# Attention of the second layer: twelve bursts on TensorE in a written order, and two multiplications on GpSimd

## The chip, the cores and the metric

The kernel runs on one core of a Trainium2 chip. The metric is the device time of one execution in microseconds, and the number for a kernel is the median of its runs. The engines are named as the profile names them: PE (TensorE matmuls), PEld (its weight loads), DVE (VectorE), ACT (ScalarE), POOL (GpSimd), SP (SyncE, which issues the loads).

## What is computed

Two decoder layers work on 256 tokens of width 1024, in float32. Layer 0 mixes tokens by causal pooling, layer 1 by causal attention with 12 heads of width 64; both layers also attend with 4 heads to a memory of 256 rows, and both end in a squared-ReLU MLP of width 4096. With 256 tokens there is one block of keys, so the block choice of the reference always takes the token's own block, and layer 1 is plain causal attention:

```python
def moba_mixer(qkv, q_gain, k_gain, cos, sin):
    q, k, v = jnp.split(qkv, 3, axis=-1)
    ...
    q = apply_rope(rms_norm(heads(q), q_gain), cos, sin)
    k = apply_rope(rms_norm(heads(k), k_gain), cos, sin)
    ...
    s_own = jnp.einsum('bhcd,bhkd->bhck', qc, k_own).astype(jnp.float32) * scale
    s_own = jnp.where(kpos[None, :] <= qpos[:, None], s_own, NEG)
    ...
    p = jax.nn.softmax(s, axis=-1).astype(v.dtype)
    ...
x = x + jnp.concatenate([tok, mo], axis=-1) @ w_out[i]
u = rms_norm(x, g_mlp[i])
x = x + jnp.square(jax.nn.relu(u @ w_ff1[i])) @ w_ff2[i]
```

## The kernel before, in words

Tokens lie on the 128 partitions in two blocks, `b` = 0 and 1. A float32 product is made of three fp32r matmuls: every operand is split into a rounded part `hi` and a rest `lo`, and `mm3` (L142 to L145) adds hi by hi, hi by lo and lo by hi into one PSUM accumulator `acc`. Weights come by DMA into `raw` (seven buffers), ACT makes `hi` (L132, or L136 with the gain as scale) and DVE makes `lo` (L133, L139); sixteen buffers of each let both run ahead of PE. The activations of layer 1 are `x2T`.

The attention of layer 1 needs five column chunks of `w_in_moba`, each 512 wide. `in_chunk` (L222) makes a chunk in eight steps, k = 0 to 7, of six matmuls (three parts by two token blocks), so a chunk is 48 matmuls. In order: chunk 2048 (values of heads 8 to 11 and memory queries), three chunks of queries and keys of four heads each (`qk_chunk(0)` to `qk_chunk(2)`), and chunk 1536 (values of heads 0 to 7). Then `wout_phase` (L391) multiplies the concatenated heads `cat` with `w_out`, 96 matmuls, the first four steps of 12 in the written order and the rest accumulator by accumulator; every finished accumulator is added to `xr` and transposed (`residual_t`, L162).

Between these projections stand small pieces of work, which `in_chunk` calls as hooks at steps that the table `PLAN` gives:

- `mem_q` (L284): four transposes of the memory queries, and their split.
- `mem_scores` (L337): 12 matmuls per token block, maximum on DVE, `exp` on ACT straight from PSUM.
- `qk_evac` (L714): after a chunk of queries and keys, for each block, squares on ACT (L202), sums on DVE (L204), the power -1/2 on POOL (`rsqrt`, L189), rotation on DVE (L722 to L726), then the keys' half of `rot` times the factors on DVE (L727), four transposes on PE (L730) and a copy to `qkT` on ACT (L731).
- `tok_scores` (L736): four score products per block for four heads; they are float32 and show as eight PE rows in the trace. `tok_probs` (L748) adds the mask and takes the maximum on DVE (L753), then calls `exp_t`.
- `exp_t` (L308): `exp` with its sum on ACT (L314), the reciprocal of the sum on DVE (L318), the probabilities times it on DVE (L321), and, held back in `pend` until `later` or `flush` calls it, transposes on PE (L327) and a copy to `pT` on ACT (L332). For four heads of the token attention that makes 8 `exp`, 8 multiplications (four of 128x128, four of 128x256) and 12 transposes.
- `av_out` (L357): probabilities times values, and the split of the result into `cat` (L150 on ACT, L151 on DVE).

`pend` holds at most `LAG` = 2 entries. All small pieces share four PSUM tiles (`psp`), the projections four accumulators (`accp`).

The order of instructions on PE, ACT, DVE and POOL is not the order of the program text: the framework's scheduler sets it when the kernel is built. Only SP (and ACT at the start) follow the program, under `manual_schedule`. Whatever the order, each engine works its own list one by one, and waits on semaphores.

Of the kernel before, what the change touches and what calls it, by code (L numbers as in the profile page):

```python
# [10 lines left out]
F32 = mybir.dt.float32  # L11
# [7 lines left out]
P = 128  # L19
# [17 lines left out]
LAG = 2  # L37

PLAN = {'x': 6, 'q': 5, 'bw': 7, 'pool': 5, 'mem0': (2, 4, 6, 6),
        'mem1': (7, 8), 'tok0': (5, 6), 'tok1': (0, 6), 'tok2': (6, 8), 'out2': 8,  # L40
        'bands': ((0, 2), (1, 1), (3, 5), (4, 4)), 'group': (2, 0, 4), 'outs': (0, 4),
        'wout0': (2, 4, 5, 6, 0, 1, 7, 3), 'wout1': (6, 7, 0, 2, 1, 4, 3, 5)}
# [11 lines left out]
def trunk(ctx: ExitStack, tc: tile.TileContext, x, mem, x_t0, x_t, mem_t, small, bands, rope, mask,  # L54
# [229 lines left out]
    def mem_q(a, b, qT):  # L284

        q = st.tile([P, MEMW], F32, tag="mq", name=nm("mq"))
        nc.scalar.activation(q, a, AF.Copy)
        ss = head_sums(a, 4)
        ps = psum("mem_q")
# [4 lines left out]
        return ss  # L294


    pend = []

    def later(fn):
        pend.append(fn)  # L300
        while len(pend) > LAG:
            pend.pop(0)()

    def flush():
        while pend:
            pend.pop(0)()

    def exp_t(pool, entries, p, nbuf, put):  # L308
# [82 lines left out]
    def wout_phase(l, order, catT, gcol):  # L391
        a = [[accum(), accum()], [accum(), accum()]]
        tail = []
        for i, k in enumerate(order):
            pieces = wout_rows(l, k, a, catT, gcol + k if gcol is not None and k < 6 else None)
# [298 lines left out]
    with tc.tile_pool(name="l1", bufs=1) as lp:  # L694
# [19 lines left out]
        def qk_evac(a, b, i):  # L714
# [12 lines left out]
            nc.vector.tensor_tensor(heads(rot[:, 256:]), heads(rot[:, 256:]), bcast(r[:, 4:], 4), op=ALU.mult)  # L727
            ps = psum("qk_evac")
            for c in range(4):
                nc.tensor.transpose(ps[:, c * P:(c + 1) * P], rot[:, c * P:(c + 1) * P], ident)  # L730
            nc.scalar.activation(qkT[:, 4 * i:4 * i + 4, b * P:(b + 1) * P],  # L731
                                 ps.rearrange("p (c t) -> p c t", c=4), AF.Copy)
# [15 lines left out]
        def tok_probs(b, h0, ps, nk, qr):  # L748
            s = lp.tile([P, 512], F32, tag="s", name=nm("s"), bufs=3)
# [8 lines left out]
            def put(pT):  # L758
                for j in range(2):
# [27 lines left out]
        steps = mem_heads(cat, mq, mk1, mqa, lp, (3, 6))
        qk_chunk(0, list(zip(PLAN['mem1'], steps)))
        steps[2]()
        for i in (1, 2):  # L790
            qk_chunk(i, list(zip(PLAN[f'tok{i - 1}'], head_scores(4 * i - 4))))
        hooks = list(zip(PLAN['tok2'], head_scores(8))) + [(PLAN['out2'], lambda: (later(lambda: tok_out(8)), flush()))]
# [102 lines left out]
```

## Time and profile before

| what | us |
|---|---|
| median of three runs (558.42 to 558.80) | 558.58 |
| the profiled execution's own time | 558.29 |
| its span, first to last instruction | 556.1 |
| busy in the span: PE | 548.4 |
| busy: DVE | 391.0 |
| busy: ACT | 358.7 |
| busy: POOL | 25.0 |

The span is what the trace covers; the profiled execution took 2.2 us more than it, outside any instruction. Busy times are unions of an engine's instructions, so overlapping instructions count once. The durations of matmuls are modelled, and consecutive ones overlap: how long one holds PE is read from the distance of two starts, not from its duration.

### The profile page before, as it was taken

The numbers are of one execution on the slowest core, as the hardware profiler recorded it, in microseconds if no ns is written. First come the engines' busy times: TensorE is split into PE (matmuls) and PEld (weight loads), VectorE is DVE, ScalarE is ACT, GpSimd is POOL, SyncE is SP. The second block draws the span as 40 slices with busy tenths as digits, with TensorE's granted clock in tenths as the row PEclk, the third lists the DMA queues.
The fourth block names the chain that finished last, engine by engine and source line by source line (L and its number), as shares of the span: only waits on it lengthen the run. The fifth ranks groups of instructions, "written<-read, shape, count | busy, mean of one in ns | idle before, by whom it ended". The sixth has DMA issues, their size and how long they took to land.

```text
span 556.1 us, 8168 instructions
## 1 busy us (share of the span) xinstructions
PE 548.4 (99%) x2883; PEld 456.5 (82%) x2883; DVE 391.0 (70%) x795; ACT 358.7 (64%) x658; POOL 25.0 (4%) x27
## 2 busy tenths in 40 slices
PE   8999999999999999999999999999999999999997
PEld 5888687888888888888877777878888888888885
DVE  5798977684764945948969999565858477485462
ACT  6889967756656566565767887657665665656510
POOL 0102100000000000000012112000000000000000
PEclk9999999999999999999999999999999999999999
DMA  8989674365736648449473344352584483663301
GB/s 285 340 303 342 217 222 147 100 200 195 250 121 233 183 153 271 139 164 292 147 234 111 103 149 130 119 169 78 176 278 124 180 281 104 222 227 118 147 0 75
DMA packets 46567, 101.93 MB, mean 183 GB/s; under 512 B 3648, under 2 KB 11584, under 8 KB 46528
## 3 DMA queue, kind: packets, MB, share of 16 engines
q1 hardware_dynamic: 46384, 101.42, 55.1%
q8 instruction: 22, 0.36, 0.3%
q14 instruction: 17, 0.14, 0.1%
q10 hardware_dynamic: 144, 0.01, 0.0%
HBM read 100.37 MB, written 1.05 MB: 182 GB/s over the span
## 4 chain that ended last, share of the span: by engine, by line
PE 91%; ACT 4%; DMA 1%; DVE 1%; POOL 1%; issue 0%; SPq 0%
PE step L448 18%; PE acc L143 18%; PE acc L144 17%; PE acc L145 17%; PE step L451 10%; PE acc L448 3%; ACT hi L136 2%; PE exp_t L327 2%; PE av_out L367 2%; PE acc L451 1%; PE tok_scores L743 1%; PE transpose L162 1%; DMA raw<-in_w_in_pool_dram 1%; POOL r L189 1%; PE qk_evac L730 1%; ACT junk L182 1%
## 5 line engine op out<-in xcount | busy, mean ns | idle before, releaser
L136 ACT ACTIVATE hi<-raw,sm 128x512 fp32r<-128x512 f32 (+1 forms) x212 | 149.2, 723 | 53.0 <-PE acc L145 28.1
L139 DVE SCALAR_TENSOR_TENSOR lo<-raw,sm,hi 128x512 fp32r<-128x512 f32 x212 | 150.6, 749 | 18.2 <-ACT hi L136 17.3
L132 ACT ACTIVATE hi<-raw 128x512 fp32r<-128x512 f32 (+1 forms) x152 | 94.2, 632 | 71.2 <-PE acc L145 63.1
L143 PE MATMUL acc<-hi,hh 128*128 128x512 f32 x256 | 99.9, 390 | 0.0
L144 PE MATMUL acc<-lo,hh 128*128 128x512 f32 x256 | 99.8, 390 | 0.0
L145 PE MATMUL acc<-hi,hl 128*128 128x512 f32 x256 | 99.8, 390 | 0.0
L133 DVE TENSOR_TENSOR lo<-raw,hi 128x512 fp32r<-128x512 f32 (+1 forms) x152 | 95.1, 689 | 0.0
L432 DVE TENSOR_TENSOR r<-step,c 128x256 f32<-128x256 f32 x56 | 23.6, 422 | 98.5 <-ACT c L431 98.5
L145 PEld LDWEIGHTS acc<-hi,hl 128*128 128x128 f32 x256 | 48.1, 188 | 10.1
L143 PEld LDWEIGHTS acc<-hi,hh 128*128 128x128 f32 x256 | 48.1, 188 | 9.5
L144 PEld LDWEIGHTS acc<-lo,hh 128*128 128x128 f32 x256 | 48.1, 188 | 9.5
L448 PE MATMUL step<-x1T,hi 128*128 128x512 f32 x224 | 51.9, 389 | 0.0
L448 PE MATMUL step<-x3T,hi 128*128 128x512 f32 x224 | 51.9, 389 | 0.0
L448 PEld LDWEIGHTS step<-x1T,hi 128*128 128x128 f32 x224 | 42.0, 188 | 8.7
L448 PEld LDWEIGHTS step<-x3T,hi 128*128 128x128 f32 x224 | 42.0, 188 | 8.7
L431 ACT ACTIVATE c<-step 128x256 f32<-128x256 f32 x56 | 21.3, 381 | 19.4 <-PE step L451 19.4
L143 PE MATMUL acc<-hi,x2T 128*128 128x512 f32 x80 | 32.2, 402 | 0.0
L145 PE MATMUL acc<-hi,x2T 128*128 128x512 f32 x80 | 31.7, 396 | 0.0
L144 PE MATMUL acc<-lo,x2T 128*128 128x512 f32 x80 | 31.6, 394 | 0.0
L451 PEld LDWEIGHTS step<-x3T,lo 128*128 128x128 f32 x224 | 27.8, 192 | 0.5
L451 PEld LDWEIGHTS step<-x1T,lo 128*128 128x128 f32 x224 | 27.8, 192 | 0.5
L451 PE MATMUL step<-x1T,lo 128*128 128x256 f32 x224 | 28.0, 283 | 0.0
(151 smaller groups left out, 755.3 us busy)
## 6 DMA issues: line engine op xcount, KB each, us to landing
raw<-in_w_ff_dram SPq DMA_DIRECT2D x128, 512.0 KB, 4.8
raw<-in_w_out_dram SPq DMA_DIRECT2D x16, 512.0 KB, 4.5
raw<-in_w_in_moba_dram SPq DMA_DIRECT2D x24, 256.0 KB, 4.5
raw<-in_w_mem_kv_dram SPq DMA_DIRECT2D x8, 512.0 KB, 5.6
raw<-in_w_in_moba_dram SPq DMA_DIRECT2D x8, 512.0 KB, 5.0
raw<-in_w_in_pool_dram SPq DMA_DIRECT2D x7, 512.0 KB, 6.3
xr<-in_x_dram SPq DMA_DIRECT2D x2, 512.0 KB, 7.5
raw<-in_mem_t_dram SPq DMA_DIRECT2D x4, 256.0 KB, 6.7
```

What stands on the lines that cost most here:

```text
L132: nc.scalar.activation(hi, raw, AF.Copy)
L133: nc.vector.tensor_tensor(lo, raw, hi.bitcast(F32), op=ALU.subtract)
L136: last_hi[0] = nc.scalar.activation(hi[:, :m], raw[:, :m], AF.Copy, scale=g)
L139: nc.vector.scalar_tensor_tensor(lo, raw, g, hi.bitcast(F32), op0=ALU.mult, op1=ALU.subtract)
L143: nc.tensor.matmul(o, a[0], b[0], start=start, stop=False)
L144: nc.tensor.matmul(o, a[0], b[1], start=False, stop=False)
L145: nc.tensor.matmul(o, a[1], b[0], start=False, stop=stop)
L327: nc.tensor.transpose(ps[:, c * P:(c + 1) * P], p[:, c * P:(c + 1) * P], ident)
L431: nc.scalar.activation(c, zs[i][:, S:], AF.Copy)
L432: nc.vector.tensor_tensor(z[:, i, :], zs[i][:, :S], c, op=ALU.add)
L448: nc.tensor.matmul(o, pieces[k][0][:, n * P:(n + 1) * P], t[2][:, k, :, :], start=k == 0, stop=False)
L451: nc.tensor.matmul(o[:, :S], pieces[k][1][:, n * P:(n + 1) * P], t[0][:, k, :], start=False, stop=k == NKC - 1)
```

## The change

PE is put under `manual_schedule` from the first chunk of layer 1's attention to its last `av_out`, so that there PE follows the program text. The text is rearranged so that the small pieces come in twelve bursts: memory query transposes (2 blocks), memory scores (both blocks), their probabilities' transposes (all four), memory `av_out`, and then for each group of four heads its query and key transposes (both blocks), its scores (both blocks), its probabilities' transposes (all four); the three token `av_out` stand in one place after the first two steps of `wout_phase`, with the last group's transposes between the first and the second. To make that possible, `qk_evac` returns its transposes as a function `turn`, `mem_q` puts its own in a list, `flush` takes a count, `LAG` becomes 16 in this part, and `s` gets a fourth buffer. The multiplication of probabilities by the inverse sums moves from DVE to POOL for the token attention (24 instructions; the memory's 8 stay on DVE), and so does the multiplication of the rotated keys by their factors (6 instructions). In the order of the output projection two late steps change places. SP's list is the same except for the two loads of those steps. ACT's and DVE's lists are still set by the scheduler.

The core of the diff:

```diff
-        'mem1': (7, 8), 'tok0': (5, 6), 'tok1': (0, 6), 'tok2': (6, 8), 'out2': 8,
+        'mem1': (2, 4, 8, 5), 'tok': (5, 7, 8), 'out': 2,
...
-        'wout0': (2, 4, 5, 6, 0, 1, 7, 3), 'wout1': (6, 7, 0, 2, 1, 4, 3, 5)}
+        'wout0': (2, 4, 5, 6, 0, 1, 7, 3), 'wout1': (6, 7, 0, 2, 1, 3, 4, 5)}
...
-    def exp_t(pool, entries, p, nbuf, put):
+    def exp_t(pool, entries, p, nbuf, put, engine=None):
...
-            nc.vector.tensor_scalar_mul(p[:, o:o + e[1]], p[:, o:o + e[1]], inv[:, i:i + 1])
+            (engine or nc.vector).tensor_scalar_mul(p[:, o:o + e[1]], p[:, o:o + e[1]], inv[:, i:i + 1])
...
+            for at, fn in hooks:
+                if at == i:
+                    fn()
             pieces = wout_rows(l, k, a, catT, gcol + k if gcol is not None and k < 6 else None)
...
-            nc.vector.tensor_tensor(heads(rot[:, 256:]), heads(rot[:, 256:]), bcast(r[:, 4:], 4), op=ALU.mult)
-            ps = psum("qk_evac")
...
+            nc.gpsimd.tensor_tensor(heads(rot[:, 256:]), heads(rot[:, 256:]), bcast(r[:, 4:], 4), op=ALU.mult)
+
+            def turn():
+                ps = psum("qk_evac")
+                for c in range(4):
+                    nc.tensor.transpose(ps[:, c * P:(c + 1) * P], rot[:, c * P:(c + 1) * P], ident)
+                nc.scalar.activation(qkT[:, 4 * i:4 * i + 4, b * P:(b + 1) * P],
+                                     ps.rearrange("p (c t) -> p c t", c=4), AF.Copy)
+
+            return turn
...
-            s = lp.tile([P, 512], F32, tag="s", name=nm("s"), bufs=3)
+            s = lp.tile([P, 512], F32, tag="s", name=nm("s"), bufs=4)
...
-                  s, 6, put)
+                  s, 6, put, nc.gpsimd)
...
+        lag[0] = 2 * NKC
+        in_turn = ExitStack()
+        in_turn.enter_context(tc.manual_schedule(engines={mybir.EngineType.PE}))
         a = in_chunk(x2T, w_in_moba[0], 2048, GMIX + 8)
...
+        mem_step = mem_heads(cat, mq, mk1, mqa, lp, (4, 6))
+        at = PLAN['mem1']
+        qk_chunk(0, [(at[0], turn_all), (at[1], lambda: (mem_step[0](), mem_step[1]())),
+                     (at[2], flush)])
+        at_turn, at_probs, at_scores = PLAN['tok']
+        qk_chunk(1, [(at[3], lambda: (mem_step[2](), flush())), (at_turn, turn_all), (at_scores, lambda: scores(0))])
+        qk_chunk(2, [(at_turn, turn_all), (at_probs, flush), (at_scores, lambda: scores(4))])
+        hooks = [(at_turn, turn_all), (at_probs, flush), (at_scores, lambda: scores(8))]
         a = in_chunk(x2T, w_in_moba[0], 1536, GMIX + 8, hooks=hooks)
...
-        for h0 in PLAN['outs']:
-            tok_out(h0)
+        def outs():
+            tok_out(0)
+            flush()
+            tok_out(4)
+            tok_out(8)
+            in_turn.close()
+
         x3T = big_t("x3T")
-        after_mix(wout_phase(1, PLAN['wout1'], cat, None), x3T)
+        after_mix(wout_phase(1, PLAN['wout1'], cat, None, [(PLAN['out'], outs)]), x3T)
```

PE has the same 2791 matmul instructions in both programs. From behind the third of the last residual transposes of layer 0 to the first residual transpose of layer 1 they are the same instructions too. In that stretch PE's list has 298 projection matmuls (234 with `x2T`, 64 with `cat`), 80 transposes (4 of `mem_q`, 24 of `qk_evac`, 52 of `exp_t`), 24 of `mem_scores`, 24 of `tok_scores` (48 rows in a trace) and 52 of `av_out` (104 rows). Before, the 298 stand in 21 runs: 42, 2, 40, 26, 2, 14, 12, 3, 8, 16, 1, 8, 33, 1, 10, 3, 1, 12, 12, 2, 50. Now they stand in 13 runs: 54, 12, 24, 30, 18, 30, 12, 6, 30, 12, 6, 24, 40. In this new list a group of four heads reads: scores, 30 projection matmuls, eight transposes of the next group's queries and keys, 12 matmuls, the 12 transposes of the group's probabilities, 6 matmuls, the next scores. The last group has 24 matmuls and the first `av_out` between its scores and its transposes.

PE at the last group's probabilities, before:

```order
L143 MATMUL acc_4077<-hi_4084,cat_3010 128x512
L144 MATMUL acc_4077<-lo_4085,cat_3010 128x512
L145 MATMUL acc_4077<-hi_4084,cat_3010 128x512
L327 MATMUL exp_t_4014<-ident,s_3978 128x128 x4
L143 MATMUL acc_4074<-hi_4102,cat_3010 128x512
L144 MATMUL acc_4074<-lo_4103,cat_3010 128x512
L327 MATMUL exp_t_4021<-ident,s_3996 128x128 x4
L367 MATMUL av_out_4028<-pT_3994,v 64x128
L367 MATMUL av_out_4028<-pT_4012,v 64x128
L367 MATMUL av_out_4028<-pT_4019,v 64x128
```

and now:

```order
L378 MATMUL av_out_4055<-pT_3699,v 64x128
L378 MATMUL av_out_4055<-pT_3706,v 64x128
L338 MATMUL exp_t_4070<-ident,s_3948 128x128 x2
L338 MATMUL exp_t_4075<-ident,s_3961 128x128 x2
L338 MATMUL exp_t_4080<-ident,s_3980 128x128 x4
L338 MATMUL exp_t_4087<-ident,s_3993 128x128 x4
L378 MATMUL av_out_4094<-pT_3909,v 64x128
L378 MATMUL av_out_4094<-pT_3914,v 64x128
```

The two float32 probability tiles were transposed singly between projection matmuls; now all four follow each other between the first and the second token `av_out`.

POOL, the powers of layer 1's queries and keys, before:

```order
L189 TENSOR_TENSOR r_3273<-sst_3271,mhalf 128x8
L189 TENSOR_TENSOR r_3295<-sst_3293,mhalf 128x8
L189 TENSOR_TENSOR r_3570<-sst_3568,mhalf 128x8
L189 TENSOR_TENSOR r_3592<-sst_3590,mhalf 128x8
L189 TENSOR_TENSOR r_3796<-sst_3794,mhalf 128x8
L189 TENSOR_TENSOR r_3818<-sst_3816,mhalf 128x8
```

and now, from the second chunk's queries and keys on:

```order
L189 TENSOR_TENSOR r_3498<-sst_3496,mhalf 128x8
L742 TENSOR_TENSOR rot_3502<-rot_3502,r_3498 128x256
L189 TENSOR_TENSOR r_3514<-sst_3512,mhalf 128x8
L742 TENSOR_TENSOR rot_3518<-rot_3518,r_3514 128x256
L332 TENSOR_SCALAR s_3530<-s_3530,inv_3539 128x128 x2
L332 TENSOR_SCALAR s_3543<-s_3543,inv_3552 128x128 x2
L332 TENSOR_SCALAR s_3562<-s_3562,inv_3571 128x256 x2
L332 TENSOR_SCALAR s_3575<-s_3575,inv_3584 128x256 x2
L189 TENSOR_TENSOR r_3724<-sst_3722,mhalf 128x8
```

Between the powers now stand two multiplications of rotated keys and eight of probabilities for each group of four heads.

ACT behind the last group's scores (`hi` are weights of the MLP to come), before:

```order
L314 ACTIVATE s_3978,sums_3984<-s_3978,nb_3982,r_3818 128x256 x2
L314 ACTIVATE s_3996,sums_4002<-s_3996,nb_4000,r_3818 128x256 x2
L136 ACTIVATE hi_4292<-raw_4290,sm 128x512
L332 ACTIVATE pT_4019<-exp_t_4014 128x512
L136 ACTIVATE hi_4296<-raw_4290,sm 128x512
L332 ACTIVATE pT_4026<-exp_t_4021 128x512
L150 ACTIVATE cat_3010<-av_out_4028 128x2x256
L150 ACTIVATE cat_3010<-av_out_4043 128x2x256
L150 ACTIVATE cat_3010<-av_out_4058 128x2x256
```

and now:

```order
L325 ACTIVATE s_3980,sums_3986<-s_3980,nb_3984,r_3740 128x256 x2
L325 ACTIVATE s_3993,sums_3999<-s_3993,nb_3997,r_3740 128x256 x2
L136 ACTIVATE hi_4295<-raw_4293,sm 128x512
L136 ACTIVATE hi_4299<-raw_4293,sm 128x512
L136 ACTIVATE hi_4305<-raw_4303,sm 128x512
L136 ACTIVATE hi_4309<-raw_4303,sm 128x512
L150 ACTIVATE cat_3010<-av_out_4055 128x2x256
L343 ACTIVATE pT_4073<-exp_t_4070 128x256
L343 ACTIVATE pT_4078<-exp_t_4075 128x256
L343 ACTIVATE pT_4085<-exp_t_4080 128x512
L343 ACTIVATE pT_4092<-exp_t_4087 128x512
```

Four conversions of MLP weights and the copy of the first `av_out` now stand between the last `exp` and the copies of the transposed probabilities, where one conversion stood.

## Rows read from the trace of the kernel before

**Rows 1.** The page, parts 1 (busy us, share, count) and 4 (chain by engine).
```profile
PE 548.4 (99%) x2883; PEld 456.5 (82%) x2883; DVE 391.0 (70%) x795; ACT 358.7 (64%) x658; POOL 25.0 (4%) x27
...
PE 91%; ACT 4%; DMA 1%; DVE 1%; POOL 1%; issue 0%; SPq 0%
```

**Rows 2.** Windows: us, busy us of each engine (instructions), PEclk, DMA share, GB/s.
```profile
272.30:366.70 94.40, 94.30 (x557) 74.40 (x555) 79.34 (x239) 68.97 (x158) 13.08 (x9) 1.00 0.47 143
...
320.00:335.00 15.00, 14.98 (x82) 11.74 (x81) 14.63 (x54) 12.93 (x35) 2.43 (x2) 1.00 0.45 140
```

**Rows 3.** Timeline of PE, attention of layer 1: start us, us, engine, line, instruction.
```profile
272.37 0.47 PE L143 MATMUL acc<-hi,x2T 128*128 128x512 f32 x1
...
272.68 0.39 PE L144 MATMUL acc<-lo,x2T 128*128 128x512 f32 x1
...
282.02 0.39 PE L291 MATMUL mem_q<-ident,mq 128*128 128x128 f32 x2
...
350.91 4.44 PE L367 MATMUL av_out<-pT,v 128*64 128x128 f32 x72
...
355.28 0.50 PE L145 MATMUL acc<-hi,cat 128*128 128x512 f32 x1
...
366.79 0.66 PE L162 MATMUL transpose<-ident,xr 128*128 128x128 f32 x4
```

**Rows 4.** Groups of PE by shape, 272.3 to 366.7: xcount | busy us, mean ns.
```profile
L143 PE MATMUL acc<-hi,x2T 128*128 128x512 f32 x78 | 31.4, 403 | 0.0
...
L143 PE MATMUL acc<-hi,cat 128*128 128x512 f32 x22 | 8.8, 398 | 0.0
```

**Rows 5.** Timeline of PE, small bursts between the projections.
```profile
292.38 0.38 PE L346 MATMUL mem_scores<-mkh,mqh 64*128 64x256 f32 x2
...
293.28 0.50 PE L143 MATMUL acc<-hi,x2T 128*128 128x512 f32 x1
...
309.67 0.72 PE L743 MATMUL tok_scores<-qkT 64*128 64x128 f32 x8
...
310.31 0.66 PE L327 MATMUL exp_t<-ident,s 128*128 128x128 f32 x4
...
326.50 1.13 PE L743 MATMUL tok_scores<-qkT 64*128 64x256 f32 x8
...
327.57 0.67 PE L327 MATMUL exp_t<-ident,s 128*128 128x128 f32 x4
...
340.86 1.09 PE L327 MATMUL exp_t<-ident,s 128*128 128x128 f32 x8
...
341.71 0.48 PE L143 MATMUL acc<-hi,x2T 128*128 128x512 f32 x1
```

**Rows 6.** Groups of ACT by shape, 272.3 to 366.7: xcount | busy us, mean ns.
```profile
L136 ACT ACTIVATE hi<-raw,sm 128x512 fp32r<-128x512 f32 x33 | 23.3, 724 | 11.6 <-PE acc L145 11.5
...
L314 ACT ACTIVATE s<-s,nb,r 128x256 f32<-128x256 f32 x12 | 7.1, 598 | 0.4 <-DVE nb L756 0.4
...
L314 ACT ACTIVATE s<-s,nb,r 128x128 f32<-128x128 f32 x12 | 5.8, 490 | 0.0
...
L150 ACT ACTIVATE cat<-av_out 128x512 fp32r<-128x512 f32 x4 | 2.4, 600 | 2.4 <-PE av_out L367 2.4
...
L332 ACT ACTIVATE pT<-exp_t 128x256 f32<-128x256 f32 x6 | 2.1, 383 | 0.8 <-PE exp_t L327 0.8
```

**Rows 7.** Groups of DVE by shape, 272.3 to 366.7: xcount | busy us, mean ns.
```profile
L321 DVE TENSOR_SCALAR s<-s,inv 128x256 f32<-128x256 f32 x20 | 6.2, 352 | 0.3
...
L321 DVE TENSOR_SCALAR s<-s,inv 128x128 f32<-128x128 f32 x12 | 2.9, 284 | 0.0
...
L727 DVE TENSOR_TENSOR rot<-rot,r 128x256 f32<-128x256 f32 x6 | 2.5, 425 | 0.0
```

**Rows 8.** Groups of POOL by shape, whole span: xcount | busy us, mean ns.
```profile
L189 POOL TENSOR_TENSOR r<-sst,mhalf 128x8 f32<-128x8 f32 x6 | 10.5, 1747 | 41.6 <-DVE sst L213 32.7 <-DVE nb L756 8.9
...
masks.py:199 POOL TENSOR_SCALAR_AFFINE_SELECT ident<-ident 128x128 f32<-128x128 f32 x1 | 0.3, 294 | 0.0
```

More of the change, by code (lines that the diff above doesn't have):

```diff
@@ L39 @@
 PLAN = {'x': 6, 'q': 5, 'bw': 7, 'pool': 5, 'mem0': (2, 4, 6, 6),
-        'mem1': (7, 8), 'tok0': (5, 6), 'tok1': (0, 6), 'tok2': (6, 8), 'out2': 8,
-        'bands': ((0, 2), (1, 1), (3, 5), (4, 4)), 'group': (2, 0, 4), 'outs': (0, 4),
-        'wout0': (2, 4, 5, 6, 0, 1, 7, 3), 'wout1': (6, 7, 0, 2, 1, 4, 3, 5)}
+        'mem1': (2, 4, 8, 5), 'tok': (5, 7, 8), 'out': 2,
+        'bands': ((0, 2), (1, 1), (3, 5), (4, 4)), 'group': (2, 0, 4),
+        'wout0': (2, 4, 5, 6, 0, 1, 7, 3), 'wout1': (6, 7, 0, 2, 1, 3, 4, 5)}
 B0 = P + 16
@@ L282, in mem_kv_finish, with mem_q @@
         return [lambda: block(0), lambda: block(1), end]
-    def mem_q(a, b, qT):
+    def mem_q(a, b, qT, hold=None):
         q = st.tile([P, MEMW], F32, tag="mq", name=nm("mq"))
@@ L288, in mem_q, with mem_qT @@
         ss = head_sums(a, 4)
+        if hold is None:
+            mem_qT(q, b, qT)
+        else:
+            hold.append(lambda: mem_qT(q, b, qT))
+        return ss
+    def mem_qT(q, b, qT):
         ps = psum("mem_q")
@@ L293, in mem_q, with flush @@
                    qT[0][:, :, b * P:(b + 1) * P], qT[1][:, :, b * P:(b + 1) * P])
-        return ss
     pend = []
+    lag = [LAG]
     def later(fn):
         pend.append(fn)
-        while len(pend) > LAG:
+        while len(pend) > lag[0]:
             pend.pop(0)()
-    def flush():
-        while pend:
+    def flush(n=None):
+        while pend and n != 0:
             pend.pop(0)()
-    def exp_t(pool, entries, p, nbuf, put):
+            n = None if n is None else n - 1
+    def exp_t(pool, entries, p, nbuf, put, engine=None):
         tot = sum(e[1] for e in entries)
@@ L389, in wout_rows, with wout_phase @@
         return ps_
-    def wout_phase(l, order, catT, gcol):
+    def wout_phase(l, order, catT, gcol, hooks=()):
         a = [[accum(), accum()], [accum(), accum()]]
@@ L762, in tok_probs, with turn_all @@
             exp_t(lp, [(s[:, j * nk:(j + 1) * nk], nk, qr[:, 2 * j:2 * j + 1], nb[:, j:j + 1]) for j in range(2)],
-                  s, 6, put)
+                  s, 6, put, nc.gpsimd)
         cat = big_t("cat")
+        lag[0] = 2 * NKC
+        in_turn = ExitStack()
+        in_turn.enter_context(tc.manual_schedule(engines={mybir.EngineType.PE}))
         a = in_chunk(x2T, w_in_moba[0], 2048, GMIX + 8)
         mq = (lp.tile([P, 2, S], F32R, tag="pT", name="mqh1", bufs=6), lp.tile([P, 2, S], F32R, tag="pT", name="mql1", bufs=6))
-        mqa = []
+        mqa, turns = [], []
         for b in range(2):
-            mqa.append(head_r(None, 4, x_e64[b], f"mq{b}", mem_q(a[b][:, 256:], b, mq)))
+            mqa.append(head_r(None, 4, x_e64[b], f"mq{b}", mem_q(a[b][:, 256:], b, mq, turns)))
             nc.scalar.activation(v[:, b, 512:], a[b][:, :256], AF.Copy, scale=x_r[b])
+        def turn_all():
+            while turns:
+                turns.pop(0)()
         def tok_out(h0):
@@ L776, in tok_out, with scores, qk_chunk @@
                                    for b in range(2)] for h in range(h0, h0 + 4)])
-        def head_scores(h0):
-            return [lambda: tok_scores(0, h0), lambda: tok_scores(1, h0)]
-        def qk_chunk(i, hooks=()):
+        def scores(h0):
+            tok_scores(0, h0)
+            tok_scores(1, h0)
+        def qk_chunk(i, hooks):
             a = in_chunk(x2T, w_in_moba[0], 256 * i, GMIX + 8, c1=768 + 256 * i, hooks=hooks)
-            for b in range(2):
-                qk_evac(a[b], b, i)
+            turns.extend(qk_evac(a[b], b, i) for b in range(2))
             after_chunk(hooks)
[L787 to L792, printed above, removed]
+        mem_step = mem_heads(cat, mq, mk1, mqa, lp, (4, 6))
[6 more added lines that the diff above has]
+        hooks = [(at_turn, turn_all), (at_probs, flush), (at_scores, lambda: scores(8))]
         a = in_chunk(x2T, w_in_moba[0], 1536, GMIX + 8, hooks=hooks)
```

4 lines of the change are left out of this document (removed).

## The prediction

> **What bounds the kernel now.** I read the page's first and fourth parts first. PE is busy 99% of the span, and 91% of the chain that ended last lies on PE, 1% on DVE and 1% on POOL [rows 1]. So the time is PE's list, and what is gained or lost in it goes one to one into the end. The windows say the same of the stretch that the change rearranges: from 272.3 to 366.7 PE is busy 94.30 of 94.40 us, DVE 79.34, ACT 68.97, POOL 13.08; between 320 and 335 DVE too is nearly full, 14.63 of 15.00 us [rows 2].
>
> But busy is not the same as useful here, because matmul durations overlap and stretch. So next comes the timeline of PE, read by the distance of starts. In a long run of projection matmuls 41 starts, from 272.68 to 282.02, take 9.34 us, 0.228 each; the first after a burst of transposes holds PE 0.31 us (272.37 to 272.68), that is 0.08 more [rows 3]. The other kinds at their best: eight transposes 0.85 us, 0.106 each (340.86 to 341.71); the 12 `mem_scores` of a block 0.90 (292.38 to 293.28); the scores of a group 0.64 for block 0 and 1.07 for block 1 (309.67 to 310.31, 326.50 to 327.57) [rows 5]; 72 rows of `av_out` 4.37, 0.061 each [rows 3].
>
> **What the stretch would take without losses.** The starts of the first projection matmul and of the first residual transpose of layer 1 are 94.42 us apart (272.37 to 366.79) [rows 3]. The work in it: 298 projection matmuls, 67.9 us (three rows of 78 as the first of [rows 4], and 22, 21 and 21 as the second); 80 transposes, 8.5; 24 `mem_scores`, 1.8; three groups of scores, 5.1; 104 rows of `av_out`, 6.3. Sum 89.6. So 4.8 us are lost now, in 21 returns to the projections (21 x 0.08 = 1.7) and, the other 3.1, in changes between small kinds and in waits for operands.
>
> **Part 1: the written order.** It removes no work; it removes interruptions. 13 runs instead of 21 leave 13 x 0.08 = 1.0 us of returns. Three changes between small kinds remain with no projection between (`av_out` to the query and key transposes, and `av_out` to `exp_t` to `av_out`); I take 0.15 each, between the 0.08 of a return and twice that, 0.5 together. The gain is at most 4.8 - 1.5 = **3.3 us**, if no burst waits. It may be nothing or a loss where one does, since PE now cannot step past a late operand. So each burst has to be asked how late its operands are.
>
> *Last group, between the two `av_out`.* Counted from the end of its scores, PE has 24 projections (5.6 us with the return), 24 rows of `av_out` (1.5) and eight transposes (0.85) before the fourth probability tile, so it stands there at 7.9. Four PSUM tiles exist; one holds the first `av_out`, three the first three probability tiles. The fourth can only be had when ACT has copied one out. ACT's list is 8 `exp` (4 x 0.490 + 4 x 0.598 = 4.4), four conversions (4 x 0.724 = 2.9), the copy of `av_out` (0.60, and not before 7.1), then the first copy of probabilities (0.38) [rows 6]. If the `exp` begin at once this lands at 8.3; if two conversions (1.4) are in front of them, at 9.7. So PE waits 0.4 to 1.8 us. I take **1.3**, in the upper half, because the `exp` also need DVE's maximum first. Behind this wait stands everything on PE.
>
> *First and second group.* From the end of the scores to the transposes of the probabilities PE has 42 projections and eight transposes, 10.6 us (42 x 0.228 + 0.85 + two returns). ACT's 8 `exp` need 4.4 of it. *Memory.* Between its scores and the transposes stand 24 projections, 5.6 us, plus 0.9 for the second block's scores, behind which the first block's `exp` run. Eight `exp` of 128x256 are 4.8 us by their nearest row [rows 6]. I take no wait in these; if the cover fails, it is about 1 us each.
>
> **Part 2: POOL's multiplications.** DVE loses 12 x 0.352 + 12 x 0.284 + 6 x 0.425 = 10.2 us [rows 7]. On the chain that is worth nothing by itself, PE covers it; it makes DVE's operands for PE earlier. POOL gets 30 instructions that the trace does not show on it. Call m the time of one 128x256 multiplication by the inverse sum. The nearest row is POOL's one-input AFFINE_SELECT, 0.294 us for 128x128 [rows 8]. If all of that is fixed, m is 0.3; if all of it goes with the columns, 0.59. The far row is the power, 1.747 us for eight columns [rows 8], 0.22 per column, which would make m 56 us; a multiplication is not a power, so I leave that end out of the range. I take m = 0.6, half of it for 128x128, and 1.5 m for the multiplication of rotated keys, which reads two operands.
>
> Is that in time? In a middle group POOL must do two powers (3.5), two key multiplications (3 m) and eight of probabilities (6 m) between the first power's operand, some 0.5 us before the end of the scores, and the last tile's transposes, which come 1.3 us after the first (12 x 0.106): 3.5 + 9 m within 10.6 + 0.5 + 1.3 = 12.4. It holds up to m = 1.0. In the last group 6 m must fit between the first `exp` and the last tile, about 6 us, again m = 1.0. At 0.6 POOL's part costs nothing.
>
> The Trainium skill speaks against this part: its page "GPSIMD Engine Reference", section "Performance versus the Vector engine", has elementwise work twice as slow there as on VectorE (2,048 columns of addition 4,497 ns against 2,293). An estimate by that page is m = 0.7, twice the 0.352 of the trace. The sum would be the same by either, as both lie under 1.0; no run so far shows which holds.
>
> **The rest costs nothing:** the deeper `pend`, the fourth `s`, the held `mem_q` and the two swapped steps of the output projection issue no instruction more, and SP keeps its order but for two loads.
>
> **Sum.** 3.3 - 1.3 = 2.0 us less. On the profiled execution's own time that is 558.29 - 2.0 = 556.3; the median of the runs is 0.29 above it, so **556.6**. About 0.2%, 1.1 us, is what a measurement can tell from no change here.
>
> **The rivals.**
>
> *No wait at all* (chance 0.13). ACT gets through the conversions early, or the PSUM tile comes free sooner: 558.6 - 3.3 = 555.3. For it: ACT was busy only 68.97 of 94.40 us [rows 2]. Against: its order behind the last `exp` is fixed.
>
> *The waits come back in the bursts* (0.17). DVE, full at 14.63 of 15 us before, still splits the weights in a list that the scheduler made; if rotation or maximum come late, the bursts of two groups wait 1 us each, and the 2.0 are gone: 558.6. For it: nothing else can run on PE meanwhile. Against: 10.2 us less for DVE.
>
> *POOL is too slow* (0.20), the one that ends on the other side. Each 1 us of m over 1.0 costs 9 + 9 + 6 = 24 us in the three groups, and swallows the 1.3 of ACT. The 3.3 are used up at m = 1.14. At m = 1.3, some two times the row's upper reading, the time is 558.6 + 7.2 - 3.3 = 562.5. Behind a late multiplication stand, on POOL, the next group's powers, and on PE the whole list. For it: no such instruction is in the trace, and DVE is nearly full while these would run. Against: the AFFINE_SELECT row. The same page of the Trainium skill, section "Specifications", says that GpSimd shares its SBUF interfaces with VectorE and contends with VectorE instructions of two SBUF inputs; by that rule m would stretch exactly where DVE makes `lo`, which reads two. No run so far shows it.
>
> That the change does not do what it says has no chance: the list of PE shows the bursts.
>
> **How the numbers follow.** The forecast has 0.50, with its own range 555.6 to 557.9 (waits 0.4 to 1.8, and 0.9 for the changes of kind and small waits that I took at nothing). Nearly all of it (0.49) and *no wait* (0.13) are faster by over 0.2%: 0.62. *Waits come back* and the rest of the forecast give 0.18 for within 0.2%; slow POOL gives 0.20 for slower. The range for 8 in 10 goes from 554.9, a little under *no wait*, to 561.0, which takes in POOL up to m = 1.24; it leaves out POOL slower than that.
>
> **What would show it.** In the profile after: projections in 13 runs; PE's starts in the stretch about 92.4 us apart in all; one wait of about 1.3 us at the fourth tile of the last group's transposes, with ACT as releaser; POOL rows of 128x256 multiplication under 1.0 us; DVE busy some 10 us less. Wrong would be: transposes of probabilities waiting for POOL (slow POOL), or `qk_evac` and `tok_scores` waiting for DVE or ACT (waits come back), or no wait in the last group at all.

## The result, and the profile after

The changed kernel takes 561.61 us (median of six runs; without the one disturbed run among them it is 561.18, of 560.58 to 562.54), the kernel before in the same comparison 558.49 (558.08 to 558.80): a ratio of 1.0055 with an interval of 1.0044 to 1.0066. It is 3.1 us slower (2.7 without that run), where 2.0 us less were forecast; 561.61 lies above the range, and the case that came is the rival on the other side, "POOL is too slow". The profiled execution took 560.84, its span is 559.0 (before 556.1).

The page's parts 1 and 4 of the changed kernel, which answer to [rows 1]:

```profile
PE 546.5 (98%) x2883; PEld 456.1 (82%) x2883; DVE 385.8 (69%) x765; ACT 357.3 (64%) x658; POOL 50.5 (9%) x57
...
PE 84%; POOL 5%; ACT 5%; DVE 3%; issue 1%; DMA 1%; POOLq 0%; SPq 0%; ACTq 0%
```

POOL is busy in 9% of the span, and yet 5% of the chain now lies on it, where 1% did. PE's share fell from 91% to 84%. A nearly idle engine has come onto the path. The timeline of PE says where (start us, duration us; answers to [rows 3, 5]; in brackets the idle time before and its releaser):

```profile
272.37 0.47 PE L143 MATMUL acc<-hi,x2T 128*128 128x512 f32 x1
...
312.45 0.50 PE L143 MATMUL acc<-hi,x2T 128*128 128x512 f32 x1
...
323.00 1.31 PE L338 MATMUL exp_t<-ident,s 128*128 128x128 f32 x8
325.50 0.44 PE L338 MATMUL exp_t<-ident,s 128*128 128x128 f32 x2 [1.19 <-POOL s L332]
326.91 0.44 PE L338 MATMUL exp_t<-ident,s 128*128 128x128 f32 x2 [0.97 <-POOL s L332]
327.10 0.48 PE L143 MATMUL acc<-hi,x2T 128*128 128x512 f32 x1
...
340.74 0.87 PE L338 MATMUL exp_t<-ident,s 128*128 128x128 f32 x6
...
345.08 0.48 PE L143 MATMUL acc<-hi,x2T 128*128 128x512 f32 x1
...
355.33 1.58 PE L338 MATMUL exp_t<-ident,s 128*128 128x128 f32 x10
357.20 0.44 PE L338 MATMUL exp_t<-ident,s 128*128 128x128 f32 x2 [0.29 <-POOL s L332]
357.57 0.66 PE L378 MATMUL av_out<-pT,v 128*64 128x128 f32 x8
...
369.58 0.66 PE L162 MATMUL transpose<-ident,xr 128*128 128x128 f32 x4
```

Twelve transposes are 1.27 us of work (12 x 0.106). The three bursts of probabilities take 4.10 (323.00 to 327.10), 4.34 (340.74 to 345.08) and 2.24 us (355.33 to 357.57), 6.9 more than three times 1.27. The stretch from 272.37 to the first residual transpose is 97.21 us, against 94.42 before: 2.79 longer, nearly the whole difference of the spans. Without these 6.9 it is shorter than forecast: 97.21 - 6.9 = 90.3, against 91.1 (the 89.6 of work and the 1.5 left). The sum of the waits of PE's weight loads for POOL agrees (us in total, times, longest):

```profile
PEld exp_t L338 <- POOL s L332: 6.9, 8, 1.4
```

POOL's groups by shape (count, busy us, mean ns; [rows 8] had none of these):

```profile
L332 POOL TENSOR_SCALAR s<-s,inv 128x256 f32<-128x256 f32 x12 | 13.3, 1126 | 0.0
...
L332 POOL TENSOR_SCALAR s<-s,inv 128x128 f32<-128x128 f32 x12 | 9.3, 789 | 8.9 <-PE acc L145 5.8 <-DVE nb L775 3.1
L742 POOL TENSOR_TENSOR rot<-rot,r 128x256 f32<-128x256 f32 x6 | 4.1, 677 | 1.5 <-DVE sst L213 0.9 <-DVE rot L741 0.4
```

One multiplication of 128x256 takes 1.126 us in the mean, where 0.6 was taken, and one of 128x128 0.789, where 0.3 was. The keys, taken at 0.9, take 0.677. POOL's timeline shows one group as a list, and three single multiplications out of the eight:

```profile
312.61 1.64 POOL L189 TENSOR_TENSOR r<-sst,mhalf 128x8 f32<-128x8 f32 x1 [8.62 <-DVE sst L213]
314.55 0.62 POOL L742 TENSOR_TENSOR rot<-rot,r 128x256 f32<-128x256 f32 x1 [0.30 <-DVE sst L213]
315.12 1.64 POOL L189 TENSOR_TENSOR r<-sst,mhalf 128x8 f32<-128x8 f32 x1
316.84 0.61 POOL L742 TENSOR_TENSOR rot<-rot,r 128x256 f32<-128x256 f32 x1
318.96 7.89 POOL L332 TENSOR_SCALAR s<-s,inv 128x128 f32<-128x128 f32 x8 [1.51 <-DVE nb L775]
...
322.90 0.92 POOL L332 TENSOR_SCALAR s<-s,inv 128x256 f32<-128x256 f32 x1
...
323.80 1.65 POOL L332 TENSOR_SCALAR s<-s,inv 128x256 f32<-128x256 f32 x1
...
325.43 1.42 POOL L332 TENSOR_SCALAR s<-s,inv 128x256 f32<-128x256 f32 x1
```

The group's scores end at 312.45. POOL works from 312.61 to 326.85 with two gaps, and is done 14.4 us after the scores; PE stood at the transposes 10.55 after them, as forecast (10.6), and could have used the last tile 1.3 later. The eight multiplications alone take 7.89. Among those of one shape and the same operands there are 0.92, 1.65 and 1.42. DVE's timeline has this beside the two long ones:

```profile
323.45 2.70 DVE L133 TENSOR_TENSOR lo<-raw,hi 128x512 fp32r<-128x512 f32 x4 [1.31 <-ACT hi L132]
```

From 323.45 to 326.15 DVE subtracts four weight tiles, two SBUF operands each. DVE's busy time fell by 5.2 us (391.0 to 385.8), where 10.2 were taken; one reason is that beside POOL some of its own instructions got longer, the small `nb` of L775 for one: 0.238 us in the mean for 0.158 before, and once 0.54 beside a multiplication of keys. So two questions were put to the chip: which part of the change costs the time, and why a multiplication takes 1.126.

### The profile page after: what moved, and what is told of

Read it like the earlier page. It is cut to its first block, busy times and chain, and to the rows that moved or that the text cites. A ratio compares the mean times of both kernels' runs of the same rounds, so it can differ in the third digit from the quotient of the medians.

```text
span 559.0 us, 8202 instructions
## 1 busy us (share of the span) xinstructions
PE 546.5 (98%) x2883; PEld 456.1 (82%) x2883; DVE 385.8 (69%) x765; ACT 357.3 (64%) x658; POOL 50.5 (9%) x57
## 4 chain that ended last, share of the span: by engine, by line
PE 84%; POOL 5%; ACT 5%; DVE 3%; issue 1%; DMA 1%; POOLq 0%; SPq 0%; ACTq 0%
PE step L463 18%; PE acc L143 16%; PE acc L144 16%; PE acc L145 16%; PE step L466 10%; POOL s L332 3%; PE acc L463 3%; ACT hi L136 2%; POOL r L189 1%; PE acc L466 1%; PE av_out L378 1%; PE transpose L162 1%; DMA raw<-in_w_in_pool_dram 1%; PE exp_t L338 1%; ACT junk L182 1%
## 5 line engine op out<-in xcount | busy, mean ns | idle before, releaser
L139 DVE SCALAR_TENSOR_TENSOR lo<-raw,sm,hi 128x512 fp32r<-128x512 f32 x212 | 150.9, 751 | 17.5 <-ACT hi L136 17.3
L143 PE MATMUL acc<-hi,hh 128*128 128x512 f32 x256 | 99.9, 390 | 0.0
L133 DVE TENSOR_TENSOR lo<-raw,hi 128x512 fp32r<-128x512 f32 (+1 forms) x152 | 95.3, 688 | 5.8 <-ACT hi L132 5.8
L143 PEld LDWEIGHTS acc<-hi,hh 128*128 128x128 f32 x256 | 48.1, 188 | 9.5
L143 PE MATMUL acc<-hi,x2T 128*128 128x512 f32 x80 | 32.2, 403 | 0.0
```

The costliest lines, as they stand in the source:

```text
L133: nc.vector.tensor_tensor(lo, raw, hi.bitcast(F32), op=ALU.subtract)
L139: nc.vector.scalar_tensor_tensor(lo, raw, g, hi.bitcast(F32), op0=ALU.mult, op1=ALU.subtract)
L143: nc.tensor.matmul(o, a[0], b[0], start=start, stop=False)
```

## The experiments

Every kernel is the changed one with the edit shown, but for the old order, which starts from the kernel before, and the later transposes, which start from the order alone. Each was timed beside the kernel before on its chip (558.04 to 558.41); ratios are to that, with 95% intervals.

**The order alone.** Both multiplications back on DVE.

```diff
-            nc.gpsimd.tensor_tensor(heads(rot[:, 256:]), heads(rot[:, 256:]), bcast(r[:, 4:], 4), op=ALU.mult)
+            nc.vector.tensor_tensor(heads(rot[:, 256:]), heads(rot[:, 256:]), bcast(r[:, 4:], 4), op=ALU.mult)
...
-                  s, 6, put, nc.gpsimd)
+                  s, 6, put)
```

> The order of the change alone: both multiplications back on DVE, POOL does the powers only, as before. Theory P: within 0.8 us of the run with only the probabilities on DVE, since POOL's key multiplication (0.61 us where nothing disturbs it) ended in time; 556 to 557.5 us. Rival W: above 558.5. Rival D (DVE, 14.6 of 15 us busy before in part of this stretch, needs the relief): DVE gets back 10.2 us of work, and the bursts wait for it by more than 1 us in all, 558 or more, though the run with the probabilities alone on DVE is faster than that.

Measured: 556.18 us (555.51 to 556.25), ratio 0.9958 [0.9946, 0.9971], 2.2 us less than before. The written order gives what was forecast for it, and POOL's part costs 561.61 - 556.18 = 5.4 (5.0 with 561.18). PE's timeline has the whole stretch and the bursts of the second and the last group:

```profile
272.21 0.48 PE L143 MATMUL acc<-hi,x2T 128*128 128x512 f32 x1
...
337.70 0.60 PE L338 MATMUL exp_t<-ident,s 128*128 128x128 f32 x4
...
339.63 0.63 PE L338 MATMUL exp_t<-ident,s 128*128 128x128 f32 x4 [0.48 <-DVE s L332]
340.01 0.47 PE L143 MATMUL acc<-hi,x2T 128*128 128x512 f32 x1
...
350.25 1.09 PE L338 MATMUL exp_t<-ident,s 128*128 128x128 f32 x8
351.62 0.66 PE L338 MATMUL exp_t<-ident,s 128*128 128x128 f32 x4 [0.28 <-ACT pT L343]
352.21 0.44 PE L378 MATMUL av_out<-pT,v 128*64 128x128 f32 x4
...
364.24 0.66 PE L162 MATMUL transpose<-ident,xr 128*128 128x128 f32 x4
```

The stretch is 92.03 us, the 90.3 without waits and 1.7 more. The second group's burst takes 2.31 instead of 1.27, 1.0 lost, mostly to DVE's multiplication, which stands between weight subtractions; the last group's takes 1.96, 0.7 lost, to ACT's copy at the fourth tile.

**Probabilities on DVE, keys on POOL.** Only the last argument of the call goes (`s, 6, put)`).

> The order of the change, with the multiplication of probabilities by the inverse sums back on DVE (24 instructions); the keys' multiplication stays on POOL. Theory P (POOL's multiplications are late: 0.79 us for 128 columns and 1.13 us for 256 in the profile of the change, and PE waited 6.9 us for them in its three bursts of transposes): those waits go, a wait for ACT of about 1.3 us may stay in the last burst, and the time is 556 to 557 us, 1.5 to 2.5 below the kernel before. Rival W (bursts in a fixed order wait whoever multiplies, because all eight multiplications now have to be done before PE goes on): PE waits for DVE instead, and the time stays above 558.5.

Measured: 557.29 us (556.67 to 558.53), ratio 0.998 [0.9971, 0.9989], 0.3 above the expected range and 1.1 above the order alone, where 0.8 at most was expected. No wait of PE for POOL is left, and the last group's burst waits for what the prediction named (waits of PE's loads):

```profile
PEld exp_t L338 <- ACT pT L343: 1.1, 1, 1.1
```

So 4.3 of the 5.4 us (3.9 of 5.0 with 561.18) go with the multiplication of probabilities. The shares of the two multiplications don't simply add up, as the next run shows.

**Keys on DVE, probabilities on POOL.** Only the first pair of lines of the first diff.

> The change with the keys' multiplication back on DVE and the probabilities' on POOL. Theory P (the eight late multiplications of a group cost, the keys' do not): they still wait behind the powers, only 2 x 0.61 us earlier in two groups, while DVE gets 2.6 us back in all; 559.5 to 562, clearly slower than the kernel before. Rival K (the keys' multiplication, which stands in front of the probabilities' on POOL, is what makes them late): under 558.5.

Measured: 563.30 us (562.93 to 563.66), ratio 1.0093 [1.0079, 1.0106], slower than the change itself and above what was expected. POOL's list is 1.2 us shorter in each group (two keys of 0.61), and the first group's multiplications still begin later, at 319.51 instead of 318.96. They need DVE's inverse sum: the group's first reciprocal starts at 319.16 here and at 318.71 in the changed kernel, and in front of it DVE has got the two multiplications of keys back. POOL's row names PE as the releaser, but the inverse sum is there only at 319.33:

```profile
319.51 8.00 POOL L332 TENSOR_SCALAR s<-s,inv 128x128 f32<-128x128 f32 x8 [2.98 <-PE acc L144]
```

So the keys on POOL were not what made it late. The windows of this kernel (us, busy us, PEclk third from the end) show a second loss, in the second group's waits and behind them:

```profile
342.00:346.00 4.00, 1.42 (x7) 0.61 (x6) 1.32 (x3) 1.88 (x5) 4.00 (x4) 1.00 0.83 285
346.00:350.00 4.00, 3.89 (x18) 2.85 (x20) 0.69 (x1) 2.52 (x5) 0.06 (x1) 0.57 0.25 70
```

PE was busy 1.42 of 4.00 us, and in the next four the granted clock is 0.57 in the mean: from 346.5 on it is 0.50, 1.2 instead of 2.4 GHz. The six projections that follow start 0.43 us apart instead of 0.228, and from the end of the burst to the end of the next scores PE needs 4.57 us (346.34 to 350.91), in the changed kernel 3.08 (345.08 to 348.16). So about 1.5 us of this run's loss are the clock's. It does not follow from the waits alone: in the changed kernel's profile PE was busy 1.61 of 4.00 us (341 to 345), and the granted clock stayed at 1.00.

**The old order with POOL's multiplications.** Both multiplications moved to POOL in the kernel before, in the scheduler's order.

```diff
-            nc.vector.tensor_scalar_mul(p[:, o:o + e[1]], p[:, o:o + e[1]], inv[:, i:i + 1])
+            (engine or nc.vector).tensor_scalar_mul(p[:, o:o + e[1]], p[:, o:o + e[1]], inv[:, i:i + 1])
...
-            nc.vector.tensor_tensor(heads(rot[:, 256:]), heads(rot[:, 256:]), bcast(r[:, 4:], 4), op=ALU.mult)
+            nc.gpsimd.tensor_tensor(heads(rot[:, 256:]), heads(rot[:, 256:]), bcast(r[:, 4:], 4), op=ALU.mult)
...
-                  s, 6, put)
+                  s, 6, put, nc.gpsimd)
```

> The kernel before with both multiplications moved to POOL and the scheduler's own order on PE. Theory P: PE waits for POOL here too, since a group's eight multiplications take 7 to 8 us on POOL and the scheduler places transposes sooner behind the scores than the change does; 3 us or more slower than the kernel before, 561.5 to 568. Rival W: only the written order is at fault, and the scheduler makes the best of POOL; within 1.1 us of the kernel before or faster.

Measured: 568.72 us (568.07 to 569.48), ratio 1.0187 [1.0173, 1.0201], 0.7 above the expected range. The waits of PE's loads, and two windows:

```profile
PEld qk_evac L730 <- POOL rot L727: 5.4, 4, 4.0
PEld exp_t L327 <- POOL s L321: 5.2, 10, 0.9
```

```profile
322.00:326.50 4.50, 0.78 (x6) 0.40 (x4) 1.92 (x3) 0.30 (x1) 4.20 (x5) 1.00 0.53 148
326.50:330.20 3.70, 3.70 (x20) 3.23 (x19) 1.68 (x11) 1.62 (x3) 0.00 (x0) 0.54 0.28 103
```

Without the written order POOL's part costs about 10 us, twice as much. POOL works its list one by one: a key multiplication stands behind four of probabilities, and PE's transposes of queries and keys wait 4.0 us for it. Not all of the 10 us are waits: PE was busy 0.78 of 4.50 us, and then the granted clock was 0.54 in the mean of 3.70 us; from 361.00 to 364.20 it was 0.51, again behind waits for POOL. By half of these two stretches, an estimate, the clock costs some 3 us. So the price of a slow engine depends on what is queued behind it, and in this kernel it is lower in the written order.

**Another form of the same multiplication.** POOL takes the inverse sums as a second operand, broadcast over the columns, instead of a per-partition scalar.

```diff
+            if engine is None:
+                nc.vector.tensor_scalar_mul(p[:, o:o + e[1]], p[:, o:o + e[1]], inv[:, i:i + 1])
+            else:
+                engine.tensor_tensor(p[:, o:o + e[1]], p[:, o:o + e[1]], inv[:, i:i + 1].to_broadcast([P, e[1]]), op=ALU.mult)
```

> The change, but POOL multiplies by the inverse sum as a two-operand instruction, the sum spread over the columns by a stride of zero, in place of the one-operand form with a scalar per partition. In the profile of the change the two-operand key multiplication took 0.613 us for 256 columns when undisturbed, the one-operand form 0.918. Theory P with the price at fault: 256 columns take 0.6 to 0.7, 128 about 0.4, eight of them some 4.2 us in place of 7.9, the waits for POOL fall under 1 us in all, and the time is 556 to 557.5. Rival C (it is VectorE's access to the same memory that stretches POOL, not the form): still 1.0 or more for 256 columns, and the time within 1 us of the change, about 561.

Measured: 556.45 us (556.38 to 556.68), ratio 0.9968 [0.9955, 0.998]. POOL's groups, and PE's wait:

```profile
L335 POOL TENSOR_TENSOR s<-s,inv 128x256 f32<-128x256 f32 x12 | 9.3, 804 | 0.0
L335 POOL TENSOR_TENSOR s<-s,inv 128x128 f32<-128x128 f32 x12 | 7.7, 668 | 8.8 <-PE acc L145 5.8 <-PE acc L144 1.6 <-DVE nb L778 1.5
```

```profile
PEld exp_t L341 <- POOL s L335: 2.8, 5, 0.9
```

The form alone takes back all but 0.3 us of the 5.4. PE still waits 2.8 us for POOL, where under 1 was expected; the order alone loses 1.7 in other waits instead. Where DVE does nothing that disturbs, one takes 0.61 us (128x256) and 0.40 (128x128), against 0.92 and 0.60 of the scalar form. Beside the subtractions of L133 these too take 1.06 to 1.15 and 0.77 to 0.92, so the means (0.804 and 0.668) are above what was expected, and the rival named a part of the truth.

**A one-operand instruction in place of the subtraction.** For the output projection's weights of layer 1, DVE makes `lo` as the upper part times zero, so this projection lacks its rest.

```diff
-            nc.vector.tensor_tensor(lo, raw, hi.bitcast(F32), op=ALU.subtract)
+            if shared:
+                nc.vector.tensor_scalar_mul(lo, hi.bitcast(F32), 0.0)
+            else:
+                nc.vector.tensor_tensor(lo, raw, hi.bitcast(F32), op=ALU.subtract)
...
-        ps_ = [split(raw[:, 0, h * 512:(h + 1) * 512], g) for h in range(2)]
+        ps_ = [split(raw[:, 0, h * 512:(h + 1) * 512], g, shared=l == 1) for h in range(2)]
```

> The change with POOL as it is, but the lower parts of layer 1's output weights are set to zero by a one-input instruction on DVE in place of the subtraction that reads two operands from SBUF (the output weights of layer 1 lose their lower parts by this). These 16 instructions lie beside POOL's multiplications; where they covered one fully in the profile of the change it took 1.42 to 1.65 us for 256 columns in place of 0.918. Theory C (two-operand work on DVE holds POOL up): the 256-column multiplications come to 0.92 to 1.0 on average, 128 columns to 0.60 to 0.65, PE's wait for POOL in the three bursts falls from 6.9 to 2 to 4 us, and the time is 557 to 559.5. Rival F (POOL's one-operand form is simply that slow and uneven): durations as before, 1.1 and 0.8, and 560.5 to 562.

Measured: 558.76 us (558.29 to 559.1), ratio 1.0008 [0.9999, 1.0017], PE's wait for POOL 4.8 us.

```profile
L335 POOL TENSOR_SCALAR s<-s,inv 128x256 f32<-128x256 f32 x12 | 12.0, 1016 | 0.0
...
L335 POOL TENSOR_SCALAR s<-s,inv 128x128 f32<-128x128 f32 x12 | 8.6, 730 | 8.6 <-DVE nb L778 8.6
```

It helped by about half: 558.76 lies in the expected range, the durations and PE's wait (expected 2 to 4) lie above theirs. DVE's `lo` became shorter (0.468 us in the mean, for 0.727), but single multiplications beside it still took 1.41 us (128x256) and 1.29 (128x128). So "two operands" was not the whole of it: either DVE's work as such disturbs, or this quick form does too.

**A reduction in place of the subtraction.** At the same places, with nearly the length of the subtraction: a reduction over one element each, which leaves a copy of the upper part (`shared` as in the last diff).

```diff
+                with nc.allow_low_precision(reason='sum of one'):
+                    nc.vector.tensor_reduce(lo, hi.bitcast(F32).unsqueeze(2), axis=AX.X, op=ALU.add)
```

> The changed kernel, in which the lower part of the output projection's weights of layer 1 (DVE's subtraction of two SBUF operands at L133, all that lie beside POOL's multiplications in the first two groups) is made by a TENSOR_REDUCE over one element each: it reads one operand, takes about as long (0.68 us for 128x512) and leaves a copy of the upper part instead of the rest, so the values of this projection change and the order does not. Theory (POOL is held where DVE does certain forms over SBUF, the two-operand subtraction and the quick one-operand multiplication of the last experiment, and not because DVE is busy): beside the reductions one multiplication takes 0.92 us (128x256) and 0.60 us (128x128), the means fall from 1.13 and 0.79 to below 0.98 and 0.65, the eight of a group from 7.9 to about 6.1, PE's wait for POOL at the probabilities' transposes from 6.9 to 1 to 3 us, and the time is 556.8 to 558.6. Rival (any pass of DVE over so many columns of SBUF holds POOL): means about 1.1 and 0.78, PE's wait 6 to 7 us, the time 560 to 562, as in the changed kernel.

Measured: 556.37 us (556.02 to 557.04), ratio 0.9969 [0.9957, 0.9982], a little under the expected range. POOL's groups, its first list, and PE's wait:

```profile
L336 POOL TENSOR_SCALAR s<-s,inv 128x256 f32<-128x256 f32 x12 | 10.9, 921 | 0.0
...
L336 POOL TENSOR_SCALAR s<-s,inv 128x128 f32<-128x128 f32 x12 | 7.3, 624 | 9.0 <-DVE mx L776 5.9 <-DVE nb L779 3.1
```

```profile
319.35 6.20 POOL L336 TENSOR_SCALAR s<-s,inv 128x128 f32<-128x128 f32 x8 [1.50 <-DVE nb L779]
```

```profile
PEld exp_t L342 <- POOL s L336: 2.2, 4, 0.7
```

All twelve multiplications of 128x256 now take 0.916 to 0.925 us, although DVE reduces beside five of them and does L139 beside three. The group takes 6.20 for 7.89. DVE's being busy does not slow POOL; certain forms do. One of the 128x128 multiplications still took 0.85 for 0.60, beside the end of an L139, a reciprocal, a small `nb` and the start of a reduction.

L139, which here has the line L143, also meets POOL, and the one that got longer is DVE. Its four instructions at the last group, here beside POOL's multiplications and in the order alone without them:

```profile
350.44 3.50 DVE L143 SCALAR_TENSOR_TENSOR lo<-raw,sm,hi 128x512 fp32r<-128x512 f32 x4 [0.45 <-ACT hi L140]
```

```profile
349.13 2.73 DVE L139 SCALAR_TENSOR_TENSOR lo<-raw,sm,hi 128x512 fp32r<-128x512 f32 x4
```

**Less for POOL.** POOL does only the twelve 128x128 multiplications, in the two-operand form; DVE has the 128x256 ones and the keys (the keys by the first pair of lines of the first diff).

```diff
-            (engine or nc.vector).tensor_scalar_mul(p[:, o:o + e[1]], p[:, o:o + e[1]], inv[:, i:i + 1])
+            if engine is None or e[1] > P:
+                nc.vector.tensor_scalar_mul(p[:, o:o + e[1]], p[:, o:o + e[1]], inv[:, i:i + 1])
+            else:
+                engine.tensor_tensor(p[:, o:o + e[1]], p[:, o:o + e[1]], inv[:, i:i + 1].to_broadcast([P, e[1]]), op=ALU.mult)
```

> A split: POOL multiplies the 12 probability tiles of 128 columns in the two-operand form (0.40 us undisturbed), DVE the 12 of 256 columns and the keys. Theory P with the price at fault: no wait for POOL, and DVE, which in the run with both on DVE made the transposes of the second group wait about 1.1 us, has 3.4 us less; 555.4 to 556.2, at or below that run (556.18). Rival: what DVE saves it waits elsewhere, 556.2 to 557.

Measured: 555.79 us (555.29 to 556.38), ratio 0.9959 [0.9946, 0.9971]: it beats both kernels, and is not to be told from the order alone (0.9958). Nothing on PE waits for POOL. The waits that are left in PE's bursts are the two of the order alone, for DVE's multiplication in the second group and for ACT's copy in the last:

```profile
339.43 0.63 PE L341 MATMUL exp_t<-ident,s 128*128 128x128 f32 x4 [0.46 <-DVE s L333]
...
351.59 0.66 PE L341 MATMUL exp_t<-ident,s 128*128 128x128 f32 x4 [0.45 <-ACT pT L346]
```

**Later transposes.** The order alone, with the last group's transposes one step of the output projection later, so that ACT has time for its copies.

```diff
-            tok_out(0)
...
-        after_mix(wout_phase(1, PLAN['wout1'], cat, None, [(PLAN['out'], outs)]), x3T)
+        after_mix(wout_phase(1, PLAN['wout1'], cat, None, [(PLAN['out'], lambda: tok_out(0)), (PLAN['out'] + 1, outs)]), x3T)
```

> Both multiplications on DVE, and the last group's transposes with the second and third av_out moved one step of the output projection later, so 12 more projection matmuls (2.8 us) lie in front of them. Theory A (the wait in the last burst is for ACT, whose list has four weight conversions in front of the copies): its 0.7 us wait goes, and the time is 555.3 to 556, below 556.18. Rival: the wait moves behind, to the split of the av_out results, which the next step of the output projection needs at once now; 556.2 to 558.

Measured: 557.05 us (556.54 to 557.49), ratio 0.998 [0.9971, 0.9989], 0.9 more than the order alone. The wait in the burst is gone: its twelve transposes now take 1.41 us (354.68 to 356.09). But the first `av_out` is now followed at once by the step that reads its result from `cat`, and PE waits longer there, for the split by ACT and DVE, as the rival said:

```profile
351.11 0.50 PE L143 MATMUL acc<-hi,cat 128*128 128x512 f32 x1 [1.07 <-ACT cat L150]
...
352.27 0.50 PE L145 MATMUL acc<-hi,cat 128*128 128x512 f32 x1 [0.43 <-DVE cat L151]
...
354.68 1.47 PE L338 MATMUL exp_t<-ident,s 128*128 128x128 f32 x12
```

## Why the prediction was wrong

- **What bounds the kernel.** Right: PE's list, one to one. The stretch grew by 2.79 us and the span by 2.9.
- **The order: 3.3 less the waits.** The sum came out, 2.2 for 2.0, but partly by luck, since two terms were off and cancel. Without waits the stretch is 90.3 us, so the order is worth 4.1 and not 3.3; and the order alone loses 1.7 in waits and not 1.3, of which 1.0 in the second group, where none was taken.
- **The last group's wait for ACT, 1.3.** Right in place, at the fourth tile; in size 1.1 with only the probabilities on DVE, and 0.7 in the order alone. In the changed kernel it does not show, because POOL's wait covers it, as the rival said.
- **The time that PE leaves for a group.** Right: 10.55 us for 10.6.
- **"I take m = 0.6."** This is the step that failed. POOL's one-input AFFINE_SELECT of [rows 8] was read as the nearest row, and its upper reading, 0.59, was taken as the top of the bounds. AFFINE_SELECT is another instruction, and its row is no bound for this one. Alone the multiplication takes 0.92 us for 128x256, and 0.60 for 128x128, where half of 0.6 was taken; beside DVE's `lo` the means are 1.126 and 0.789. The estimate by the Trainium skill's page "GPSIMD Engine Reference", section "Performance versus the Vector engine", 0.7, was too low as well. Half for the small tile failed with it: at m = 1.126 the prediction's own line, 24 us for each 1 us over 1.0, gives 558.6 + 3.0 - 3.3 = 558.3, inside its range. What carries the time out is that 128x128 costs 0.789 and not half of 1.126.
- **"It holds up to m = 1.0."** Right, though by two errors that cancel: the keys were taken at 1.5 m and measured 0.677, and the 1.5 us in which POOL waits for DVE's `nb` before the first multiplication were left out. Six times m stands for four of each shape; in these units the runs give: two operands (4 x 0.804 + 4 x 0.668) / 6 = 0.98 and 556.45 us; the reduction 1.03 and 556.37; the quick form 1.16 and 558.76; the changed kernel 1.28 and 561.61. Undisturbed, (4 x 0.92 + 4 x 0.60) / 6 = 1.01 lies just at the edge. Up to about 1.03 POOL costs next to nothing beyond the other waits of the order, and from there (561.61 - 556.37) / (1.28 - 1.03) = 21 us per 1 us (19 with 561.18), where 24 were worked out.
- **The rival "POOL is too slow".** It came, with its time: 562.5 was given for m = 1.3, and 561.61 measured at 1.28. Its mechanism stood there, the late multiplications and the stretching beside `lo`. The section "Specifications" of the Trainium skill's page "GPSIMD Engine Reference" has contention with DVE instructions "in a 2-port perf mode or with two SBUF inputs". The traces agree in part: the subtraction of L133 stretches POOL (up to 1.65 for 0.92); L139, which also reads two SBUF tiles, left three multiplications at 0.92 in the reduction's run, where it got longer itself, and stretched one to 1.16 in the changed kernel. The quick one-operand form stretched POOL too. What failed was its chance of 0.20, which rested on the AFFINE_SELECT row alone. With m open between 0.6 and what contention may add, 1.0 was not far off.
- **The range.** It ended at m = 1.24, and the chip gave 1.28 in the units above.

What stays open: what ACT and DVE would do with a list written by hand, since the waits of 0.7 and 1.0 that are left in the order alone move when the list changes; and what decides, when POOL and a form of DVE meet, which of the two gets longer: with POOL's scalar form it was mostly POOL beside L133, and mostly DVE beside L139.

## What to carry to other kernels

A nearly idle engine is no free engine: before work is moved to it, time the exact instruction form there, and ask beside which instructions of the other engines it will run. Work out the duration at which the move turns into a loss, as a number per instance, and give the chance by how far the unknown price may lie from it, not by the nearest row of another operation. When order and engine change together, try the order alone first: here all of the gain was in it.

## What was not expected of the hardware

- On POOL the multiplication by a per-partition scalar is slower than that by a second operand: 0.92 against 0.61 us for 128x256, 0.60 against 0.40 for 128x128.
- POOL's instructions get longer beside certain DVE forms: 1.65 for 0.92 beside the two-operand subtraction (1.79 with the keys on DVE), 1.41 beside the quick one-operand multiplication. Beside DVE's reductions they do not (0.92).
- DVE can be the one that gets longer: four L139 took 3.50 us beside POOL's scalar form, 2.73 without, and POOL's three multiplications stayed at 0.92. The subtraction, 0.687 us before, took 0.727 in the mean in the changed kernel and 0.788 beside POOL's two-operand form. That two-operand form does lose to L139 too: 0.99 instead of 0.61 for the keys.
- With the keys on DVE, PE was busy 1.42 of 4.00 us in one group's waits, and the granted clock then stood at 1.2 GHz for some 3 us: there a late operand cost more than its wait. In the changed kernel's profile it did not happen. Its other runs may differ by the same (560.58 at a mean clock of 0.999, 562.54 at 0.996), but no trace of those is kept.
